# A third early pair of output tiles, another turn of the operand pools, and an earlier row-factor chain in a two-layer diffusion backbone

## The chip, the core and the metric

One core of one Trainium2 chip runs the whole kernel. The metric is device time in microseconds (us), the median of several runs. TensorE is called PE in the rows, VectorE DVE, ScalarE ACT, GpSimd POOL, and SyncE, which issues most transfers, SP.

## The reference

512 latent tokens and 256 context tokens of width 1024 pass through two layers. Layer 0 mixes tokens by windowed attention, layer 1 by a bidirectional gated linear recurrence over 8 heads of width 128. Each layer ends in a gated channel mixer of width 2816 (FFN0, FFN1). Everything is float32. After the recurrence, which is what the change touches, it computes, shortened:

```python
o = rms_norm(ox_f + flip(ox_b), o_gain) * silu(gate)      # per head of 128
x = x + g1 * (o.reshape(512, 1024) @ w_out)
h = rms_norm(x, norm2_g) * (1 + sc2) + sh2
gate, val = split(h @ w_up)                               # 1024 -> 2 x 2816
x = x + g2 * ((silu(dwconv3(gate)) * val) @ w_down)
```

## The kernel before

Activations lie transposed, features on the 128 partitions and tokens along the free axis. Each float32 product is made of three matmuls, with operands split into a rounded high part and the rest: `wh`*high, `wh`*low, `wl`*high. `mm_steps` (line 170) issues these three for each of the 8 feature blocks `k`.

**Weights.** `load_w` brings raw weights into one of two raw tiles of 1 MB (`wr`, transfers on SP's queue, line 95). Blocks of 512 columns are then converted, the high part by ScalarE (line 117), the rest by VectorE (line 118), into a pair of operand tiles (`wh`, `wl`). The pair comes from a list of pools, `self.wsp`, which is used in turn: `operand` takes the first pool and moves it to the end. `ws0` has 4 slots, `wsC`, `wsD` and `wsE` have 2 each. Conversions are issued with a higher priority than the program's order gives them.

**Recurrence.** For head `h`, `front` makes forget gates and queries, `back` values and gate, `scan` the recurrence. `scan` is a generator; between its steps the matmul steps of `back(h)` and `front(h+1)` are taken as filling. Behind head 7 the filling is `begin_out`: the output projection `ho` for tile pairs (0, 4) and (1, 5), each over heads 0 to 6 only, since head 7 isn't ready. A pair takes one of two double-bank tiles of pool `pj`. The scan's own banks are pool `sc` (`at`, `po`, `oss`, `oR`) and pool `lv` (`lv`, the fifth blocks of `kT` and `U`), two each. The end of a head is a chain: transposes `kT`, products `U`, states `S` on VectorE, outputs `po`, squares `osq` on ScalarE, sums `oss`, `rv` on VectorE, a power on POOL, `dg`, the broadcast `oR`, the product `oT`, and the split into `oh` by ScalarE and VectorE.

**Output projection and FFN1.** `hgrn_out` adds head 7 to the first two pairs and makes pairs (2, 6) and (3, 7) whole. Each tile is added to the stream by VectorE (`add_gated`, line 895), then scaled into `hn` (lines 362 and 363), squared (line 513) and added up in `acc` on POOL (line 515). FFN1 begins with `gate_plain` for its first block of 128 columns: 48 matmuls `pd` for the gate, 48 for the value, both without the row factor 1/rms. The generator `row_factor` makes that factor: first `nss` (sums over partitions of `acc`), `rv` and POOL's power, then `dg`, the broadcast `nR` and the copy into `R`. VectorE multiplies with `R` when it reads the products.

**Order.** The program gives each instruction a priority by its place. The builder's planner makes one fixed queue for each engine from that, before the run: an instruction that is ready by the planner's own time may pass one that isn't.

Of the kernel before, what the change touches and what calls it, by code (L numbers as in the profile page):

```python
# [8 lines left out]
F32 = mybir.dt.float32  # L9
# [7 lines left out]
P = 128  # L17
D = 1024
KT = D // P
# [53 lines left out]
class Kernel:  # L73
# [824 lines left out]
    def gate_plain(self, ft, ops, hn, G, gg, R, rows, half, tmp, bank):  # L898


        nc = self.nc
        act = lambda k: (hn[:, 0, k], hn[:, 1, k])
        cols = ((0, 256), (256, C0))
        for j, dst in enumerate((G[:, 1:1 + C0], gg)):
            ps = [bank("pd")[:, 0:hi - lo] for lo, hi in cols]
            for _ in self.mm_steps(ops[j], range(KT), act, [(o, lo) for o, (lo, _) in zip(ps, cols)]):
                pass
            for _ in rows:
                pass

            for o, (lo, hi) in zip(ps, cols):
                nc.vector.tensor_tensor(dst[:, lo:hi], o, R[:, lo:hi], op=ALU.mult)
# [119 lines left out]
    def hgrn(self, hn, R, acc, hb, pj, lv, sc):  # L1032
        nc, a = self.nc, self.a
        win = a["hgrn_w_in"][0]
        act = lambda k: (hn[:, 0, k], hn[:, 1, k])
        es = ExitStack()
# [7 lines left out]
        rows = self.row_factor(acc, False, h1, sc, "sc", 512, R, 1.0, (h1, "dg"))  # L1044
# [188 lines left out]
        wout = a["hgrn_w_out"][0]  # L1233
        part = [None, [], []]

        def split_o(h):
            oh = part[0]
            nc.scalar.activation(oh[:, 0, h], oT[:, h], AF.Copy)
            nc.vector.tensor_tensor(oh[:, 1, h], oT[:, h], f(oh[:, 0, h]), op=ALU.subtract)

        def begin_out():

            part[0] = oh = hb.tile([P, 2, KT, LAT], F32R, tag="hn", name="oh1")
            for dp in range(2):
                w = self.load_w([self.wcols(wout, d * P, P) for d in (dp, dp + 4)])
                ps = pj.tile([P, 1024], F32, tag="pj", name="ho")
                part[1].append(w)
                part[2].append(ps)
                for j in range(2):
                    out = [(ps[:, 512 * j:512 * j + 512], 0)]  # L1250
                    for k in range(KT - 1):
                        if dp == 0 and j == 0:
                            split_o(k)
                        yield from self.mm_steps(w[j], (k,), lambda k: (oh[:, 0, k], oh[:, 1, k]), out, k == 0, False)
# [4 lines left out]
        for h in range(KT):  # L1259
            def fill(h=h):  # L1260
                yield from back(h, ss[h])
                yield from (front(h + 1, ss[h + 1]) if h + 1 < KT else begin_out())

            rest = fill()
            for n in scan(h, ss[h]):
                for _ in range(n):
                    next(rest, None)
            for _ in rest:
                pass
# [4 lines left out]
    def hgrn_out(self, part, hn, acc, tmp, pj):  # L1274
        nc = self.nc
        self.shifts(1, 1, hn)
        wout = self.a["hgrn_w_out"][0]
        oh = part[0]
        act = lambda k: (oh[:, 0, k], oh[:, 1, k])
        for dp in range(KT // 2):  # L1280
            if dp < 2:
                w, ps, ks = part[1][dp], part[2][dp], (KT - 1,)
            else:
                w = self.load_w([self.wcols(wout, d * P, P) for d in (dp, dp + 4)])
                ps = pj.tile([P, 1024], F32, tag="pj", name="ho")
                ks = range(KT)
            for j in range(2):
                d = dp + 4 * j
                pd = ps[:, 512 * j:512 * j + 512]
                for _ in self.mm_steps(w[j], ks, act, [(pd, 0)], first=dp >= 2):  # L1290
                    pass
                self.add_gated(1, 2, d, pd, True)
            for d in (dp, dp + 4):
                self.scaled(1, 1, d, hn, True)
                self.square_acc(d, acc, True, tmp, "sg", first=(d == 0), eng=nc.gpsimd)
# [6 lines left out]
    def run(self, stop=99):  # L1302
        nc, a = self.nc, self.a
        top = ExitStack()
# [11 lines left out]

        xp = self.pool(top, "xp")
        self.xl = xp.tile([P, KT, LAT], F32, tag="xl", name="xl")
        self.wsp.append(self.pool(top, "wsC", 2))
        Rp = self.pool(top, "Rp", 1)  # L1320
        pjs = ExitStack()
        pj = self.pool(pjs, "pj", 2, PSUM)
# [6 lines left out]
        es = ExitStack()  # L1329
# [17 lines left out]
        rows = self.row_factor(acc, False, tmp, bk, "ps", 512, R, -1.0, (gp, "g"))  # L1347
# [23 lines left out]
        pjs.close()  # L1371
        pj = self.pool(pjs, "pj", 2, PSUM)
        es = ExitStack()
        self.wsp.append(self.pool(top, "wsD", 2, right=True))
        e2 = ExitStack()
        sc = self.pool(e2, "sc", 2, PSUM)
        lv = self.pool(e2, "lv", 2, PSUM)
        part = self.hgrn(hn2[0], R, accs[0], hb, pj, lv, sc)
# [13 lines left out]
        es = ExitStack()  # L1392
        tmp = self.pool(es, "tmpB", 2)
        acp = self.pool(es, "accB", 1)
        gp = self.pool(es, "gpB", 9)
        self.wsp.append(self.pool(es, "wsE", 2))
        bk = self.pool(es, "bkB", 8, PSUM)
        rows = self.row_factor(acc, True, tmp, bk, "ps", 512, R, -1.0, (gp, "g"))
        ost = {}
# [53 lines left out]
```

## Time and profile before

| | us |
|---|---|
| median of 3 runs | 1876.24 (1875.39 to 1877.27) |
| profiled execution | 1872.88 |
| its span, first to last instruction | 1871.1 |
| mean granted TensorE clock | 0.988 |

The span is what the rows of the trace lie in; the profiled execution's time is the number to which a sum of rows belongs, and the median is what a changed kernel is compared with. Times in rows are us from the span's start.

### The profile page before, as it was taken

To read this page: it belongs to the slowest core of one execution; us is meant where nothing else is said; L and a number is where in the kernel's file an instruction comes from. 1 tells how busy PE (TensorE), PEld (TensorE's weight loads), DVE (VectorE), ACT (ScalarE), POOL (GpSimd) and SP (SyncE) were. 2 spreads that over 40 slices of the span, in tenths; PEclk is the share of its full clock that TensorE was granted. 3 is DMA by queue.
4 is the path that set the end of the run, shared out by engine and by line. 5 is a ranking of instruction groups with operands and counts; after the bars stand their busy time and mean duration, and the time that the engine had idled before them with its cause. 6 is when DMAs were issued, how large, how long until landed. Compare 5 with 4: busy or idle time off the path is not lost.

```text
span 1871.1 us, 32302 instructions
## 1 busy us (share of the span) xinstructions
PE 1801.3 (96%) x13326; PEld 1576.9 (84%) x13326; DVE 1214.1 (65%) x2243; ACT 754.7 (40%) x1478; POOL 247.4 (13%) x233
## 2 busy tenths in 40 slices
PE   6999999998999999999998999999998999999998
PEld 4976786787888888989887888988886799899997
DVE  5575667466867686766777676777676655455462
ACT  4354555465534252434354333333332443233332
POOL 1233333103201000101013101111110200000000
PEclk9999999998999999999998999999999999999999
DMA  9204104232333333233313212122220332333321
GB/s 309 66 23 158 47 24 169 68 102 68 124 113 102 113 124 113 91 113 124 113 61 90 58 35 58 35 57 58 57 69 24 90 91 91 90 96 96 92 82 65
DMA packets 204416, 166.44 MB, mean 89 GB/s; under 512 B 5149, under 2 KB 198254, under 8 KB 199150
## 3 DMA queue, kind: packets, MB, share of 16 engines
q1 hardware_dynamic: 196608, 160.47, 27.8%
q10 hardware_dynamic: 7662, 3.92, 0.7%
q8 instruction: 105, 1.72, 0.4%
q14 instruction: 41, 0.34, 0.1%
HBM read 162.27 MB, written 2.10 MB: 88 GB/s over the span
## 4 chain that ended last, share of the span: by engine, by line
PE 87%; DVE 5%; DMA 4%; issue 2%; ACT 1%; POOL 1%; SPq 0%; ACTq 0%; POOLq 0%; DVEq 0%
PE dn L170 15%; PE pd L170 13%; PE pZ L188 8%; PE pf L170 8%; PE pV L188 4%; PE pjq L598 4%; PE pv L170 4%; PE ao L170 4%; PE ho L170 3%; PE pq L170 3%; PE pv L824 2%; PE pt L816 2%; PE ada L309 2%; PE pY L188 2%; PE pgate L170 2%; PE kv L598 2%
## 5 line engine op out<-in xcount | busy, mean ns | idle before, releaser
L117 ACT ACTIVATE wh<-wr 128x512 fp32r<-128x512 f32 (+1 forms) x320 | 193.0, 618 | 452.3 <-DMA wr<-in_ffn_w_up 74.8
L118 DVE TENSOR_TENSOR wl<-wr,wh 128x512 fp32r<-128x512 f32 (+1 forms) x320 | 223.6, 705 | 140.3 <-ACT wh L117 138.3
L170 PE MATMUL dn<-g,wh 128*128 128x512 f32 (+1 forms) x1056 | 263.3, 357 | 2.2 <-ACT g L995 2.2
L170 PE MATMUL pd<-hn,wh 128*128 128x256 f32 (+1 forms) x1408 | 227.3, 284 | 0.9 <-issue 0.9
L170 PEld LDWEIGHTS dn<-g,wh 128*128 128x128 f32 x1056 | 175.4, 189 | 32.7 <-ACT g L995 2.8
L170 PEld LDWEIGHTS pd<-hn,wh 128*128 128x128 f32 x1408 | 194.2, 190 | 2.5 <-issue 2.3
L188 PE MATMUL pZ<-hs,wh 128*128 128x386 f32 x704 | 185.2, 345 | 3.0 <-ACT wh L140 1.5
L170 PE MATMUL dn<-g,wl 128*128 128x512 f32 (+1 forms) x528 | 159.4, 356 | 0.0
L140 ACT ACTIVATE wh<-wr 128x512 fp32r<-128x512 f32 x132 | 81.6, 628 | 167.9 <-DMA wr<-in_ffn_w_up 47.4
L170 PE MATMUL pd<-hn,wl 128*128 128x256 f32 x704 | 141.8, 283 | 0.0
L188 PEld LDWEIGHTS pZ<-hs,wh 128*128 128x128 f32 x704 | 128.0, 190 | 15.7 <-ACT wh L140 4.4
L141 DVE TENSOR_TENSOR wl<-wr,wh 128x512 fp32r<-128x512 f32 x132 | 94.0, 717 | 53.6 <-ACT wh L140 53.5
L170 PE MATMUL pf<-hn,wh 128*128 128x512 f32 (+1 forms) x512 | 119.3, 349 | 9.7 <-DVE xc L1023 8.8
L188 PE MATMUL pZ<-hs,wl 128*128 128x386 f32 x352 | 119.4, 343 | 2.2 <-DVE wl L141 2.2
L926 POOL TENSOR_TENSOR gg<-gg,R 128x772 f32<-128x772 f32 x22 | 53.9, 2449 | 458.3 <-DVE gg L925 446.6
L170 PEld LDWEIGHTS pd<-hn,wl 128*128 128x128 f32 x704 | 109.0, 190 | 0.0
L1023 DVE SCALAR_TENSOR_TENSOR xl<-dn,mod,xl 128x512 f32<-128x512 f32 x72 | 53.9, 748 | 73.7 <-PE dn L170 73.6
L170 PEld LDWEIGHTS dn<-g,wl 128*128 128x128 f32 x528 | 87.4, 188 | 14.8
L170 PEld LDWEIGHTS pf<-hn,wh 128*128 128x128 f32 x512 | 80.9, 192 | 22.5 <-ACT wh L117 9.1
L188 PE MATMUL pV<-hs,wh 128*128 128x386 f32 x352 | 92.2, 341 | 5.0 <-ACT hs L392 5.0
L598 PE MATMUL pjq<-wh,hn 128*128 128x256 f32 x384 | 77.8, 291 | 0.0
L188 PEld LDWEIGHTS pZ<-hs,wl 128*128 128x128 f32 x352 | 66.7, 190 | 6.6 <-DVE gg L925 3.4
(299 smaller groups left out, 3807.1 us busy)
## 6 DMA issues: line engine op xcount, KB each, us to landing
wr<-in_ffn_w_up SPq DMA_DIRECT2D x88, 512.0 KB, 5.1
wada<-in_ada_w SPq DMA_DIRECT2D x40, 1024.0 KB, 4.8
wr<-in_hgrn_w_in SPq DMA_DIRECT2D x40, 512.0 KB, 4.2
ar<-in_ada_w SPq DMA_DIRECT2D x32, 256.0 KB, 7.1
wr<-in_ffn_w_down SPq DMA_DIRECT2D x16, 512.0 KB, 4.1
wr<-in_ffn_w_down SPq DMA_DIRECT2D x8, 896.0 KB, 4.7
wr<-in_attn_w_in SPq DMA_DIRECT2D x6, 1024.0 KB, 8.1
wr<-in_attn_w_out SPq DMA_DIRECT2D x8, 512.0 KB, 4.9
```

What stands on the lines that cost most here:

```text
L117: nc.scalar.activation(wh, src, AF.Copy)
L118: nc.vector.tensor_tensor(wl, src, f(wh), op=ALU.subtract)
L140: nc.scalar.activation(ops[i][0], src, AF.Copy)
L141: nc.vector.tensor_tensor(ops[i][1], src, f(ops[i][0]), op=ALU.subtract)
L170: nc.tensor.matmul(o, lhsT=wt, rhs=at[:, t0:t0 + o.shape[1]], start=(first and n == 0 and i == 0), stop=(last and n == len(ks) - 1 and i = ...
L188: self.nc.tensor.matmul(ps, lhsT=wt, rhs=at, start=(first and k == 0 and i == 0), stop=(k == nk - 1 and i == 2), skip_group_check=not first)
L309: nc.tensor.matmul(ps[32 * j:32 * j + 32, 0:512], lhsT=self.cs[:, k, :], rhs=raw[:, j * 512:(j + 1) * 512], start=(k == 0), stop=(k == KT ...
L598: nc.tensor.matmul(out, lhsT=x, rhs=y[:, wk], start=(start and k == 0 and j == 0), stop=(stop and k == KT - 1 and j == 2))
L816: nc.tensor.transpose(pt[:, j * P:(j + 1) * P], pr[j][:, b * P:(b + 1) * P], self.ident)
L824: nc.tensor.matmul(pv[a * HD:(a + 1) * HD, 0:256], lhsT=V[:, tl, g, :], rhs=pT[:, a * 256:(a + 1) * 256], start=(b == 0), stop=(b == len(t ...
L926: times = lambda eng, o, x, y: eng.tensor_tensor(o, x, y, op=ALU.mult)
L1023: nc.vector.scalar_tensor_tensor(x[:, d], o, self.modc(l, v, 5, d), x[:, d], op0=ALU.mult, op1=ALU.add)
```

## The change

Three edits. First, `begin_out` offers a third pair of tiles, (2, 6), over heads 0 to 3 only. Its two tiles go to two tiles of pool `lv`, its weights of heads 0 to 3 are loaded by themselves, and their operands come from `ws0` alone. `hgrn_out` loads the weights of heads 4 to 7 and completes the pair in the same banks. Second, the turn of the operand pools is set anew: `[ws0, wsC, ws0, wsD]` for the recurrence instead of `ws0, wsC, wsD`, and `wsE` behind these for FFN1. Third, `gate_plain` takes the first step of `row_factor` before its matmuls instead of behind the gate's.

```diff
@@ gate_plain
             ps = [bank("pd")[:, 0:hi - lo] for lo, hi in cols]
+            next(rows, None)
             for _ in self.mm_steps(ops[j], range(KT), act, [(o, lo) for o, (lo, _) in zip(ps, cols)]):
@@ begin_out
-            for dp in range(2):
-                w = self.load_w([self.wcols(wout, d * P, P) for d in (dp, dp + 4)])
-                ps = pj.tile([P, 1024], F32, tag="pj", name="ho")
+            for dp in range(3):
+                cols = [self.wcols(wout, d * P, P) for d in (dp, dp + 4)]
+                if dp < 2:
+                    w = self.load_w(cols)
+                    ps = pj.tile([P, 1024], F32, tag="pj", name="ho")
+                    ps = [ps[:, 0:512], ps[:, 512:1024]]
+                else:
+                    every, self.wsp = self.wsp, [self.ws0]
+                    w = [[op] for op in self.load_w([c[:, 0:4] for c in cols])[0]]
+                    self.wsp = every
+                    ps = [lv.tile([P, 512], F32, tag="lv", name="hol") for _ in range(2)]
...
-                    for k in range(KT - 1):
+                    for k in range(KT - 1 if dp < 2 else 4):
@@ hgrn_out
+            cols = [self.wcols(wout, d * P, P) for d in (dp, dp + 4)]
             if dp < 2:
                 w, ps, ks = part[1][dp], part[2][dp], (KT - 1,)
+            elif dp == 2:
+                w = [first + [op] for first, op in zip(part[1][dp], self.load_w([c[:, 4:8] for c in cols])[0])]
+                ps, ks = part[2][dp], range(4, KT)
             else:
...
-                for _ in self.mm_steps(w[j], ks, act, [(pd, 0)], first=dp >= 2):
+                for _ in self.mm_steps(w[j], ks, act, [(ps[j], 0)], first=dp >= 3):
@@ run
-        self.wsp.append(self.pool(top, "wsC", 2))
+        wsC = self.pool(top, "wsC", 2)
+        self.wsp.append(wsC)
...
-        self.wsp.append(self.pool(top, "wsD", 2, right=True))
+        wsD = self.pool(top, "wsD", 2, right=True)
+        self.wsp = [self.ws0, wsC, self.ws0, wsD]
...
-        self.wsp.append(self.pool(es, "wsE", 2))
+        self.wsp = [self.ws0, wsC, self.ws0, wsD, self.pool(es, "wsE", 2)]
```

## Rows read from the trace of the kernel before

**Rows 1.** The page, busy time in us, share of the span and instructions.

```profile
PE 1801.3 (96%) x13326; PEld 1576.9 (84%) x13326; DVE 1214.1 (65%) x2243; ACT 754.7 (40%) x1478; POOL 247.4 (13%) x233
```

**Rows 2.** Windows by stage: length, busy us of each engine, granted clock, DMA share.

```profile
1355.00:1406.00 51.00, 51.00 (x527) 45.67 (x526) 34.89 (x62) 17.26 (x36) 5.78 (x5) 1.00 0.22 63
...
1434.00:1450.00 16.00, 10.33 (x66) 7.66 (x64) 7.26 (x20) 2.65 (x6) 1.01 (x1) 0.86 0.00 1
1450.00:1480.00 30.00, 28.60 (x108) 21.54 (x108) 23.17 (x29) 15.89 (x29) 9.10 (x6) 0.90 0.38 105
1480.00:1500.00 20.00, 16.70 (x121) 15.57 (x121) 9.27 (x20) 7.61 (x11) 2.30 (x2) 0.91 0.19 54
1500.00:1600.00 100.00, 100.00 (x798) 98.21 (x798) 59.84 (x118) 38.56 (x60) 0.00 (x0) 1.00 0.32 96
...
1800.00:1871.00 71.00, 65.63 (x391) 57.32 (x390) 25.88 (x48) 18.13 (x31) 0.00 (x0) 0.99 0.21 69
```

**Rows 3.** Windows, the two seams cut finer, columns as in rows 2.

```profile
1434.00:1438.20 4.20, 4.02 (x32) 3.36 (x30) 3.23 (x11) 1.42 (x4) 0.00 (x0) 1.00 0.00 0
1438.20:1442.60 4.40, 3.21 (x24) 2.83 (x24) 1.74 (x6) 0.00 (x0) 0.00 (x0) 1.00 0.02 4
1442.60:1444.40 1.80, 1.05 (x8) 0.97 (x8) 0.78 (x2) 0.60 (x1) 0.00 (x0) 1.00 0.00 0
1444.40:1446.50 2.10, 0.00 (x0) 0.00 (x0) 0.83 (x2) 0.00 (x0) 1.01 (x1) 0.80 0.00 0
1446.50:1448.60 2.10, 2.04 (x2) 0.50 (x2) 0.00 (x0) 0.00 (x0) 0.00 (x0) 0.50 0.00 0
1448.60:1450.00 1.40, 0.00 (x0) 0.00 (x0) 0.69 (x1) 0.63 (x1) 0.00 (x0) 0.50 0.00 0
1450.00:1455.70 5.70, 5.66 (x12) 3.60 (x12) 4.42 (x9) 3.22 (x7) 0.00 (x0) 0.50 0.02 6
1455.70:1472.90 17.20, 17.17 (x73) 13.51 (x72) 12.90 (x15) 8.73 (x15) 5.82 (x4) 0.99 0.43 120
1472.90:1480.10 7.20, 5.84 (x24) 4.43 (x24) 5.85 (x7) 4.04 (x8) 3.27 (x2) 1.00 0.53 146
...
1487.80:1490.10 2.30, 0.00 (x0) 0.01 (x1) 1.04 (x3) 0.00 (x0) 1.02 (x1) 0.98 0.00 0
1490.10:1493.30 3.20, 3.18 (x9) 2.17 (x10) 0.47 (x2) 0.60 (x1) 0.00 (x0) 0.50 0.00 0
```

**Rows 4.** Windows, the instructions of tile ho alone.

```profile
1400.00:1434.00 34.00, 20.27 (x84) 15.47 (x84) 0.00 (x0) 1.00 0.18 51
```

**Rows 5.** Timeline of PE: start, us, line, operation, count, idle before.

```profile
1396.68 0.28 PE L1132 MATMUL lv<-Q,Y 128*32 128x32 f32 x6
...
1407.73 1.10 PE L546 MATMUL oR<-dg,cst 128*128 128x512 f32 x2 [0.42 <-DVE dg L543]
1408.67 1.05 PE L1113 MATMUL at<-q,KK 128*128 128x128 f32 x8
...
1446.55 2.04 PE L546 MATMUL oR<-dg,cst 128*128 128x512 f32 x2 [2.22 <-DVE dg L543]
...
1480.96 0.72 PE L170 MATMUL pd<-hn,wh 128*128 128x256 f32 x4 [0.89 <-issue]
```

**Rows 6.** Groups of VectorE by line, 1450 to 1482.5: busy us, mean ns, idle before.

```profile
L118 DVE TENSOR_TENSOR wl<-wr,wh 128x512 fp32r<-128x512 f32 x13 | 10.9, 847 | 4.4 <-ACT wh L117 4.4
L363 DVE SCALAR_TENSOR_TENSOR hn<-xl,gs,hn 128x512 fp32r<-128x512 f32 x8 | 8.6, 1079 | 0.2 <-ACT hn L362 0.2
L895 DVE SCALAR_TENSOR_TENSOR xl<-ho,mod,xl 128x512 f32<-128x512 f32 x8 | 5.9, 747 | 2.0 <-PE ho L170 1.8
```

**Rows 7.** Timelines of VectorE and of POOL, columns as in rows 5.

```profile
1455.59 0.74 DVE L363 SCALAR_TENSOR_TENSOR hn<-xl,gs,hn 128x512 fp32r<-128x512 f32 x1
...
1482.29 1.29 POOL L515 TENSOR_TENSOR acc<-acc,sq 128x512 f32<-128x512 f32 x1 [4.09 <-ACT sq L513]
```

**Rows 8.** Waits, 1098 to 1400: us in total, times, longest.

```profile
ACT wh L117 <- DMA wr<-in_hgrn_w_in: 42.7, 15, 5.7
```

More of the change, by code (lines that the diff above doesn't have):

```diff
@@ L1249, in begin_out @@
                 for j in range(2):
-                    out = [(ps[:, 512 * j:512 * j + 512], 0)]
-                    for k in range(KT - 1):
+                    out = [(ps[j], 0)]
+                    for k in range(KT - 1 if dp < 2 else 4):
                         if dp == 0 and j == 0:
@@ L1280, in hgrn_out @@
         for dp in range(KT // 2):
+            cols = [self.wcols(wout, d * P, P) for d in (dp, dp + 4)]
             if dp < 2:
                 w, ps, ks = part[1][dp], part[2][dp], (KT - 1,)
+            elif dp == 2:
+                w = [first + [op] for first, op in zip(part[1][dp], self.load_w([c[:, 4:8] for c in cols])[0])]
+                ps, ks = part[2][dp], range(4, KT)
             else:
-                w = self.load_w([self.wcols(wout, d * P, P) for d in (dp, dp + 4)])
+                w = self.load_w(cols)
                 ps = pj.tile([P, 1024], F32, tag="pj", name="ho")
+                ps = [ps[:, 0:512], ps[:, 512:1024]]
                 ks = range(KT)
@@ L1288, in hgrn_out @@
                 d = dp + 4 * j
-                pd = ps[:, 512 * j:512 * j + 512]
-                for _ in self.mm_steps(w[j], ks, act, [(pd, 0)], first=dp >= 2):
+                for _ in self.mm_steps(w[j], ks, act, [(ps[j], 0)], first=dp >= 3):
                     pass
-                self.add_gated(1, 2, d, pd, True)
+                self.add_gated(1, 2, d, ps[j], True)
             for d in (dp, dp + 4):
```

## The prediction

> **What bounds the kernel now.** The page comes first: TensorE is busy 96% of the span [rows 1]. A share that high is an average, so the stages come next. In the middle of the recurrence and in FFN1's body TensorE has no idle time at all: 51.00 of 51 us in a head, 100.00 of 100 us in FFN1 [rows 2]. Nothing that only starts operands earlier can gain there. Two seams are left: from 1434 to 1480 us, the end of the recurrence and its output projection, and from 1480 to 1493 us, the start of FFN1. FFN1's end (65.63 of 71 us busy) is not touched.
>
> The windows cut finer show what the two seams lose [rows 3]. Window less busy time is TensorE's idle time: 0.18 + 1.19 + 0.75 + 2.10 + 0.06 + 1.40 = 5.68 us from 1434 to 1450. That is head 7's last chain: states, `po`, square, row sums, POOL's power, `dg`, the broadcast `oR`, `oT`, the split into `oh`. Each link waits for the one before, and TensorE has nothing else left, because the 84 matmuls that `begin_out` offers (2 pairs x 2 tiles x 7 heads x 3) all ran before 1434 [rows 4]. The granted clock then falls: 0.80, then 0.50 from 1446.5 to 1455.7, the lower of its two levels, 1.2 GHz. So `oR` takes 2.04 us where head 6's took 1.10 [rows 5], 0.94 more, and 12 `ho` matmuls take 5.70 us. At the higher clock 73 of them take 17.20 us, 0.236 each [rows 3], so these 12 lose 5.70 - 2.83 = 2.87. The last 24 take 7.20 where 5.65 would do: 1.55 more, with a wait in front of them. The whole seam loses 5.68 + 0.94 + 2.87 + 1.55 = 11.0 us.
>
> The second seam: after the first 48 `pd` and the row sums `nss`, TensorE idles 2.30 us until `dg` is made, and the next 3.20 us run at 0.50 [rows 3], half of it lost: 1.6. Together 3.9 us.
>
> **The change, part by part.** *Third pair.* The work of `ho` does not change: 24 of its matmuls (2 tiles x 4 heads x 3), 24 x 0.236 = 5.65 us, may now run before head 7 is done. Two banks of `lv` receive them. These come free only after head 7's `U` tiles are read, if tiles of one tag are handed out in program order. The rows say so: `at` of head 7, ahead of its `lv` products in the program, ran at 1408.67, behind head 6's `oR`, while those products ran from 1396.68 on [rows 5]. Tag `sc` was the difference: `oR` stood first in its queue. So the third pair can't take a bank from the scan; it can start near 1438 us and finds 5.50 us of idle time in the five windows from 1438.2 to 1450.
>
> How much of 5.65 is hidden? At the most all; at the least 1.19, the gap in the state chain, if everything is put in it and the 4.46 left over pushes the chain back. The order of TensorE's queue is fixed beforehand, and the 84 matmuls were put as early as possible: they end at 1434 with 0.18 us idle behind them. I therefore let the first bank's 12 (2.83 us) go into the 1.19 us gap, 1.64 too much, and add 0.4 for the next gap of 0.75: the chain is late by 2.0, and 5.65 - 2.0 = 3.6 is hidden. Late behind it are `oss`, POOL's power, `dg` and `oR`, in that order, and then the last head's split.
>
> Busy gaps keep the clock up, which returns up to 0.94 at `oR` (taken) and up to 2.87 at the 12 matmuls (half taken, 1.4: 2 to 4 us of idle time may remain in front of them). Of the 1.55 I take half, 0.8: one wait for an eviction goes with the third pair's bank, one may stay. Sum of this part: 3.6 + 0.9 + 1.4 + 0.8 = 6.7 us; ends 1.2 (only the state gap is filled) and 11.0.
>
> Its loads: the pair's 1 MB is now two raw tiles of 0.5 MB each, so one more turn in a ring of two, with the same bytes; two transfers of 512 KB become four of 256 KB on SP's queue. FFN1's first raw tile then waits behind the second half, as it waited behind the whole. From 1455.7 to 1472.9 the DMA engines are 0.43 busy [rows 3]: I cost this at nothing; without that cover it is some us late, for operands that `pd` needs only behind the 84 `ho` that are left (84 x 0.236 = 19.8 us).
>
> *Operand pools in another turn.* Three pools with 4 + 2 + 2 slots in plain turn give a depth of 6 (the 2-slot pools come round every third operand); `ws0` taken twice gives 8, and 10 instead of 8 in FFN1. No matmul, conversion or byte is added. Cost and gain zero in the heads and FFN1's body, where TensorE has no idle time to give; the cover is TensorE's own backlog. The same turn leaves `ws0` free of the eight held operands' last halves, so the third pair's conversions need not wait.
>
> *1/rms chain sooner.* `nss`, `rv`, POOL's power now precede the gate's 48 `pd` in the program. At best the 3.9 us vanish: the chain runs under `pd`'s 5.7 us. At worst `nss` stands first in TensorE's queue and waits for POOL's last `acc`, 1482.29 + 1.29 = 1483.58 [rows 7], while `pd` could start at 1480.96 [rows 5]: 2.6 us lost with 48 `pd` queued behind it, 1.3 left. The lower end is not excluded, as a planned time may be early; `ho` passing unready work speaks for the upper. I take the middle, 2.6.
>
> Sum: 6.7 + 0 + 2.6 = 9.3 us. The profiled execution took 1872.88 us, 1.78 around its span of 1871.1, so it would take 1863.6. The median of the runs lies 3.36 above the profiled one: 1876.24 - 9.3 = **1866.9 us**.
>
> **The rivals.** *VectorE becomes the bound of the projection.* From 1450 to 1482.5 its three main groups take 10.9 + 8.6 + 5.9 = 25.4 us [rows 6]. Three conversions move ahead of 1450 (3 x 0.85): 22.9 remain. From the first eviction, 1452.4 as reckoned, with the 2.0 us it waits for TensorE, that is 1477.3 against 1482.5: 5.2 instead of 6.7, and 1876.24 - 5.2 - 2.6 = 1868.4. For it: L363 takes 1.08 us in the mean but 0.74 where POOL is idle [rows 6, 7], and POOL's adds crowd into a shorter stage. Against it: FFN1's conversions can slip.
> The Trainium skill (SBUF — State Buffer, Who interferes with whom) says that a VectorE instruction with two SBUF inputs contends with a GpSimd one that reads SBUF, and the loser fully blocks; L363 and POOL's add are such, and the trace agrees with its 1.08 against 0.74 us. By that rule the time would be this rival's 1868.4 rather than 1866.9.
>
> *The change doesn't do what it says*: the 24 matmuls stay behind the chain, or push it back by their own length. Then the first part is worth 1.2 to 1.5 and the sum 2.8 to 4.1: 1872.1 to 1873.4. For it: the planned gaps need not be the chip's. Against it: 84 such matmuls did move.
>
> *Slower*: deeper operands put ScalarE's conversions ahead of their data. From 1098 to 1400 us ScalarE already stood 42.7 us in 15 waits, the longest 5.7, for the recurrence's weights [rows 8]; the scan's `Y` and `kbt` queue behind such a wait, then TensorE. It is hidden today. It decides once a head costs (9.3 + 3.75) / 8 = 1.6 us of TensorE time; at 1.7 in each of 8 heads: 1866.9 + 13.6 = 1880.5. Against it: a raw tile freed sooner is also loaded sooner.
>
> **How the numbers follow.** A run of this kernel can tell about 0.2%, 3.75 us, from no change. Forecast 0.54, VectorE 0.14, no real fill 0.20, slower 0.08, smaller losses that cancel 0.04. Of the third case 0.08 still lies below 1872.5. So faster 0.54 + 0.14 + 0.08 = 0.76, same 0.12 + 0.04 = 0.16, slower 0.08. Low end: both parts at their best, 11.0 + 3.9 = 14.9, so 1861.5. High end: the third case's far end, 1873.5. Outside lie the slower case and the rarest mixes.
>
> **What would show it.** Right: `ho` matmuls between `U` and `oR`; `oR` near 1.1 us; the clock above 0.5 through the first `ho` of the last head; fewer than 90 `ho` after it; `nss` inside the first 48 `pd` and `nR` close behind them at full clock. Wrong: `po` or `oss` starting over 3 us later after `U` than now (overfilled); TensorE idle with VectorE full in the projection; `nss` ahead of `pd` behind a wait; idle TensorE inside a head.

## The result, and the profile after

The changed kernel took 1883.67 us (median of 8 runs, 1880.59 to 1887.68) against 1876.74 for the kernel before (8 runs, 1874.97 to 1879.46): a ratio of 1.0037, 95% interval 1.0028 to 1.0046. It is slower by 7 us; forecast were 9.3 us less, so the sign was wrong. Its profiled execution took 1880.59 us with a span of 1878.6.

TensorE does the same work in the same busy time. The page, as in [rows 1]:

```profile
PE 1802.4 (96%) x13326; PEld 1578.5 (84%) x13326; DVE 1217.7 (65%) x2243; ACT 756.9 (40%) x1478; POOL 251.1 (13%) x233
```

Windows over the two seams and FFN1's body, columns as in [rows 2]:

```profile
1434.00:1455.50 21.50, 16.85 (x113) 13.86 (x110) 9.20 (x22) 2.65 (x6) 1.01 (x1) 1.00 0.00 1
...
1456.40:1470.10 13.70, 13.66 (x51) 10.37 (x51) 12.11 (x19) 10.35 (x20) 3.35 (x2) 0.90 0.55 153
1470.10:1477.70 7.60, 0.00 (x0) 0.00 (x0) 7.60 (x8) 3.27 (x6) 4.53 (x4) 0.68 0.50 139
1477.70:1486.00 8.30, 8.25 (x24) 6.23 (x24) 2.56 (x4) 2.04 (x4) 1.58 (x1) 0.67 0.00 0
1486.00:1491.00 5.00, 1.48 (x10) 1.45 (x9) 2.29 (x5) 1.71 (x3) 1.26 (x1) 0.89 0.44 129
1491.00:1496.20 5.20, 5.20 (x25) 5.20 (x26) 0.85 (x2) 0.13 (x1) 1.02 (x1) 0.50 0.32 81
...
1510.00:1600.00 90.00, 90.00 (x746) 89.60 (x745) 56.36 (x111) 34.82 (x55) 0.00 (x0) 1.00 0.31 94
```

The chain of head 7 now runs at the higher clock up to the end of `oR`, but in the middle of the projection TensorE does nothing for 7.60 us while VectorE is full (7.60 of 7.60), and FFN1's first products run at 0.50. Two of these stretches are in the waits of TensorE, 1395 to 1510 (us in total, times, longest):

```profile
PE ho L170 <- DVE xl L895: 7.7, 1, 7.7
PE nss L524 <- POOL acc L515: 3.5, 1, 3.5
PE oR L546 <- DVE dg L543: 2.2, 1, 2.2
PE kT L1183 <- DVE K L1158: 1.7, 1, 1.7
```

The timeline of TensorE, columns as in [rows 5]:

```profile
1440.66 0.72 PE L170 MATMUL hol<-oh,wh 128*128 128x512 f32 x2
...
1445.41 0.40 PE L170 MATMUL hol<-oh,wl 128*128 128x512 f32 x1
1445.65 0.38 PE L1215 MATMUL po<-Q,S 128*128 128x128 f32 x2
...
1447.80 0.72 PE L170 MATMUL hol<-oh,wh 128*128 128x512 f32 x2
...
1450.68 0.95 PE L1226 MATMUL oss<-cst,osq 128*128 128x2 f32 x8
1453.85 1.10 PE L546 MATMUL oR<-dg,cst 128*128 128x512 f32 x2 [2.22 <-DVE dg L543]
1456.39 1.22 PE L170 MATMUL ho<-oh,wh 128*128 128x512 f32 x2 [1.44 <-ACT oh L1239]
...
1477.75 1.22 PE L170 MATMUL ho<-oh,wh 128*128 128x512 f32 x2 [7.66 <-DVE xl L895]
...
1489.56 1.55 PE L524 MATMUL nss<-cst,acc 128*128 128x2 f32 x8 [3.52 <-POOL acc L515]
1490.97 1.21 PE L170 MATMUL pd<-hn,wh 128*128 128x256 f32 x4
```

Between the first `po` and the next stand 21 `hol` products (1440.66 to 1445.65), and 12 more between the last `po` and `oss`: 33, not 24: nine of the 18 products for heads 4 to 6 of the pair, which the program has behind the chain, came along. The planner must have taken them as ready; e6 below, where they stand later in the program, has 24. `oR` takes 1.10 us again instead of 2.04 [rows 5].

Where an instruction stands on the clock of the span differs between profiles even where kernels agree: `at` of head 7 lies anywhere from 1432.2 to 1441.6 us, also among kernels that equal the one before up to there. So stretches are measured from that `at` (the last one in the program). Its row and that of `oss` in the kernel before:

```profile
1432.31 0.22 PE L1147 MATMUL at<-Q,K 128*64 128x64 f32 x1
...
1443.28 1.05 PE L1225 MATMUL oss<-cst,osq 128*128 128x2 f32 x8 [0.69 <-ACT osq L1219]
```

and the same `at` in the changed kernel, whose `oss` is shown above:

```profile
1434.27 0.22 PE L1148 MATMUL at<-Q,K 128*64 128x64 f32 x1
```

In us, worked out from the timelines (e1 to e16 are the experiments below): the chain is from `at` to the end of `oT`; the projection from there to the end of the last product into an output tile; "products in the chain" and "left behind it" count products into output tiles (in the first, of the third pair alone); "hn" is the mean ns of L363, "conv" that of L118, in the projection and just behind it; "first to 96th `pd`" is from start to start.

| kernel | median | ratio (95%) | products in the chain | chain | left behind it | projection, TensorE idle in it | conv, hn | to first `pd` | first to 96th `pd` | `at` to end |
|---|---|---|---|---|---|---|---|---|---|---|
| before | 1876.74 | 1 | 0 | 17.0 | 108 | 30.7, 2.1 | 847, 1079 | 0.9 | 17.3 | 438.8 |
| after | 1883.67 | 1.0037 (1.0028–1.0046) | 33 | 21.4 | 75 | 30.4, 8.4 | 932, 923 | 4.9 | 14.9 | 444.4 |
| e1 | 1877.85 | 1.0002 (0.9993–1.0011) | 0 | 17.0 | 108 | 30.7, 2.2 | 841, 1081 | 5.3 | 14.1 | 439.9 |
| e2 | 1879.72 | 1.0013 (1.0005–1.0022) | 0 | 16.4 | 108 | 33.2, 3.3 | 789, 1261 | 1.0 | 17.2 | 440.7 |
| e3 | 1881.86 | 1.0023 (1.0012–1.0034) | 42 | 23.5 | 66 | 30.1, 7.6 | 878, 1133 | 0.9 | 17.3 | 445.2 |
| e4 | 1883.85 | 1.0034 (1.0021–1.0047) | 33 | 22.3 | 75 | 30.2, 7.3 | 932, 921 | 1.0 | 17.4 | 443.7 |
| e5 | 1882.21 | 1.0035 (1.0021–1.0048) | 33 | 22.3 | 75 | 18.5, 0 | 937, 946 | 16.1 | 15.0 | 444.7 |
| e6 | 1881.83 | 1.0031 (1.0014–1.0047) | 24 | 19.7 | 84 | 29.8, 6.4 | 848, 1002 | 5.3 | 14.2 | 441.7 |
| e7 | 1872.45 | 0.9982 (0.9973–0.9991) | 0 | 17.0 | 108 | 30.7, 2.1 | 838, 1081 | 1.2 | 13.2 | 434.9 |
| e9 | 1882.29 | 1.0033 (1.0020–1.0046) | 42 | 23.5 | 66 | 30.4, 8.6 | 878, 1130 | 0.9 | 17.3 | 445.4 |
| e10 | 1876.62 | 1.0000 (0.9989–1.0011) | 33 | 21.4 | 75 | 30.3, 8.4 | 930, 919 | 1.0 | 13.2 | 438.8 |
| e11 | 1875.75 | 1.0000 (0.9991–1.0009) | 33 | 21.4 | 75 | 23.3, 2.5 | 687, 748 | 4.7 | 13.6 | 435.4 |
| e12 | 1878.58 | 1.0016 (1.0006–1.0027) | 0 | 16.1 | 108 | 35.5, 1.7 | 687, 749 | 3.4 | 13.9 | 441.4 |
| e13 | 1875.82 | 1.0002 (0.9993–1.0011) | 0 | 17.0 | 108 | 30.8, 2.1 | 688, 748 | 0.9 | 17.4 | 438.7 |
| e14 | 1873.64 | 0.9985 (0.9975–0.9994) | 12 | 17.1 | 96 | 31.8, 4.8 | 917, 922 | 0.9 | 13.2 | 435.9 |
| e15 | 1869.75 | 0.9976 (0.9966–0.9985) | 0 | 17.0 | 108 | 29.1, 0.9 | 687, 749 | 1.9 | 13.2 | 433.8 |
| e16 | 1867.75 | 0.9961 (0.9949–0.9973) | 12 | 16.5 | 96 | 26.9, 1.7 | 683, 744 | 0.9 | 13.2 | 430.0 |

After minus before, piece by piece: chain +4.4, projection -0.3, to the first `pd` +4.0, the first 96 `pd` -2.4, the rest -0.1, in all +5.6 of the 6.9 between the medians. One profile of a kernel may lie some us beside its median (3.9 below it in the kernel before, 6.6 above it in e13), so the last 1.3 us are not placed. Each experiment has its own runs of the kernel before beside it (medians 1876.15 to 1876.86), to which its ratio belongs.

### The profile page after: what moved, and what is told of

Its sections match the earlier page's. It is cut to its first block, busy times and chain, and to the rows that moved or that the text cites. A ratio compares the mean times of both kernels' runs of the same rounds, so it can differ in the third digit from the quotient of the medians.

```text
span 1878.6 us, 32348 instructions
## 1 busy us (share of the span) xinstructions
PE 1802.4 (96%) x13326; PEld 1578.5 (84%) x13326; DVE 1217.7 (65%) x2243; ACT 756.9 (40%) x1478; POOL 251.1 (13%) x233
## 4 chain that ended last, share of the span: by engine, by line
PE 87%; DVE 5%; DMA 4%; issue 2%; ACT 1%; POOL 0%; SPq 0%; ACTq 0%; DVEq 0%; POOLq 0%
PE dn L170 15%; PE pd L170 14%; PE pZ L188 8%; PE pf L170 8%; PE pV L188 4%; PE pjq L598 4%; PE pv L170 4%; PE ao L170 4%; PE pgate L170 3%; PE pq L170 3%; PE pv L824 2%; PE pt L816 2%; PE ada L309 2%; PE pY L188 2%; PE kv L598 2%; PE ho L170 2%
## 5 line engine op out<-in xcount | busy, mean ns | idle before, releaser
L118 DVE TENSOR_TENSOR wl<-wr,wh 128x512 fp32r<-128x512 f32 (+1 forms) x320 | 227.2, 715 | 133.5 <-ACT wh L117 120.7
```

What stands on the lines that cost most here:

```text
L118: nc.vector.tensor_tensor(wl, src, f(wh), op=ALU.subtract)
```

## The experiments

**The three edits alone, and two together.** e1_chain_only is the edit of `gate_plain` in the kernel before; e2_turn_only the three lines that set the turn of the pools; e3_pair_only the third pair with the old turn; e4_pair_and_turn the changed kernel without the edit of `gate_plain`.

> The kernel before with the earlier start of the 1/rms chain alone. Theory (the row sums stand first in TensorE's queue and hold the gate's 48 products back until GpSimd's last addition is done): the gate's products start some 3.7 us later than before, the idle time in front of the broadcast is gone, and the kernel is 0 to 2 us slower. Rival (the chain runs hidden under the products, as forecast): 2.6 to 3.9 us faster.

> The kernel before with the new turn of the operand pools alone. Theory (operands that are ready sooner let the planner put more projection products in front of the last head's upper levels, and the head's chain is pushed back): the heads 1 us faster in sum, the transposes of the last head 2 us later than before, the kernel 1 to 3 us slower. Rival (the turn costs and gives nothing): within 1 us of before.

> The kernel before with the third pair alone, in the old turn of the pools. Theory (the fill is put into the first two gaps of the chain, more than they hold, and afterwards the last pair's second tile waits for the eviction of its first, with nothing else left for TensorE): head 7's last products start 4 to 7 us later than before, one idle time of over 3 us stands in the middle of the last pair, and the kernel is 0 to 5 us slower. Rival (the third pair is a gain and another edit spoils it): 4 to 7 us faster.

> The changed kernel without the earlier start of the 1/rms chain. Theory (the chain's edit is worth only 1 to 2 us of the loss; most lies in the last head and in the wait of the last pair): 4 to 6 us slower than before. Rival (the row sums at the head of the queue are what costs): within 1 us of before.

No edit gains. 1.0002, 1.0013 and 1.0023 multiply to 1.0038, the changed kernel's 1.0037: within the intervals the loss is the sum of the edits, most of it the pair's. It doesn't follow that each does the same in company: the pair alone has 42 products in the chain, with the new turn 33. The pair's 5.0 us (1881.86 - 1876.86) lie at the end of the 0 to 5 expected, with one wait of 4.5 us for `xl`; e4 lost 7.0, more than the 4 to 6. In e2 the size came, but not at the place that its theory named: from `at` to `oss` there are 10.97 us as before, and the projection is 2.5 us longer. The eight `hn` take 1261 ns there instead of 1079, one more conversion stands in the stretch, and TensorE waits 2.6 us for `xl`; that these make all of the 2.5 isn't shown. In e1 `nss` stands first in TensorE's queue and `pd` waits behind it; waits of TensorE in e1:

```profile
PE nss L524 <- POOL acc L515: 3.5, 1, 3.5
```

**e5_last_pair_apart: the long wait taken away.** The 7.66 us end when `xl` has taken up a product: the last pair's two halves are one tile, and the second half's products wait until the first half has been read. In e5 they get two banks of the scan.

```diff
-                ps = pj.tile([P, 1024], F32, tag="pj", name="ho")
-                ps = [ps[:, 0:512], ps[:, 512:1024]]
+                ps = [sc.tile([P, 512], F32, tag="sc", name="hos") for _ in range(2)]
```

> The changed kernel, with the last pair's two output tiles in two banks of their own (the scan's sc banks) instead of the two halves of one tile. Theory (the second half's products wait for the eviction of the first half because both are one tile, and that eviction stands in VectorE's queue behind FFN1's conversions): the wait of 7.7 us in the middle of the last pair goes, and the low clock behind it; 4 to 8 us faster than the changed kernel, near the kernel before. Rival (VectorE alone sets the pace, and the products would only wait elsewhere): within 2 us of the changed kernel, with the idle time moved to the start of FFN1.

```profile
PE nss L524 <- POOL acc L515: 14.3, 1, 14.3
```

The rival held. The products end 12 us sooner (18.5 us without a gap), and the whole time stays within 2 us: TensorE waits 14.3 us at `nss` instead, because POOL's last addition ends 32.8 us behind `oT`, against 33.8 in the changed kernel. The long wait was where the delay showed, not its cause. e8_apart_only, the same edit in the kernel before, gave 1876.47 (1.0002, 0.9992 to 1.0012); there the wait of 1.4 us went, as its theory had it, another grew from 0.9 to 2.1, and the expected 1 to 2 us don't show in the medians.

> The kernel before with its last output pair in two banks of their own instead of the halves of one tile, nothing else. Theory (the wait of 1.4 us in front of the last tile is for the eviction of its other half): that wait is gone, 1 to 2 us faster. Rival (it waits for an operand's conversion): the wait stays, no change.

**e6_fill_capped and e9_half_pair: fewer products in the chain.** In e6 the pair's heads 4 to 6 come behind head 7's in the program, so that only the 24 are ready early. In e9 (the kernel before) only the first of the pair's tiles is offered early. The edit of e6:

```diff
-                ps, ks = part[2][dp], range(4, KT)
+                ps, ks = part[2][dp], (KT - 1, *range(4, KT - 1))
```

> The changed kernel, where the third pair's second part begins with head 7, so that only its 24 products of heads 0 to 3 can go into the last head's chain, not 33. Theory (every product beyond what a gap holds pushes the chain back by its own length, and pays for itself later): head 7's first output products start 2 us sooner than in the changed kernel; the total stays within 2 us of it, since the 9 products come back behind the chain. Rival (pushing the chain back is itself the loss): 2 us or more faster than the changed kernel.

> The kernel before with only the first of the third pair's two tiles offered early (12 products, heads 0 to 3) and the second made whole at the end; old turn of the pools, old place of the row factor. Theory (products put between the links of head 7's chain push it back, and each costs its place): the pair alone cost 5.1 us (1881.86 against 1876.8) with 42 of its products in the chain, so with some half of them about 2.5 us: 1879, and the first projection product of head 7 some 3 us later behind U than in the kernel before. Rival (the pair costs by its split operands or its late second part): as the whole pair, 1881.9, or, if only the second tile costs, no change.

e9 didn't change what it was meant to: its second tile, which no longer stood in the fill, was ready as well, and the planner put 42 products into the chain as in e3. It costs what e3 costs, so it tells nothing of half a pair. e6 does: `oss` stands 10.97 us behind `at` with none in the chain (before), 14.30 with 24, 16.41 with 33 (after), 18.51 with 42 (e3). From 24 on, nine more cost 2.1 us, 0.234 each: the full length of a product (0.236). The gaps swallowed 24 x 0.236 - 3.33 = 2.33 us, some ten products. e6's time, 1.8 us under the changed kernel's, lies too near the 2 us that were to part its theory from its rival, and the intervals overlap; the chain is 1.7 us shorter. The projection stays at some 30 us whether 108, 84, 75 or 66 products are left behind the chain.

**e7_sums_under_both and e10_sums_in_after: the second seam.** The first step of `row_factor` stands behind the second of eight blocks of the gate's products, and the rest, with the reads that need it, behind the value's. e7 is the kernel before with it, e10 the changed one (the edit shortened, arguments left out at `...`).

```diff
-            for _ in self.mm_steps(ops[j], range(KT), act, ...):
-                pass
+            for k, _ in enumerate(self.mm_steps(ops[j], range(KT), act, ...)):
+                if k == 1:
+                    next(rows, None)
+            done.append((dst, ps))
+            if ft == 0 and j == 0:
+                continue
             for _ in rows:
                 pass
-            for o, (lo, hi) in zip(ps, cols):
+            for dst, ps in done:
+                for o, (lo, hi) in zip(ps, cols):
```

> The kernel before, where the row sums follow the gate's second feature block in the program, and for the first block of FFN1 the rest of the 1/rms chain follows the value's products too, so that both halves' products can cover it. Theory (the chain's price at the start of FFN1 is the idle time in front of the broadcast and the low clock behind it; the edit failed because the row sums came first): the idle time of 2.4 us is gone, the clock stays at its higher level, 3 to 4 us faster than before. Rival (the products' banks or VectorE's reading of them take the time back): within 1 us.

> The changed kernel with the row factor's first step behind the second of the gate's eight blocks, and the rest of it behind the value's products. Theory (the seam at FFN1's start is a loss by itself, apart from the projection): 1883.7 - 4.4, what the same edit gave to the kernel before, = 1879.3, pd starting some 3 us sooner behind the projection and without the wait for POOL's sum. Rival (the projection's end, paced by VectorE, decides alone, since hn is late either way): 1883.7.

The time at FFN1's start was there to be had: 4.4 us in e7 (1876.83 - 1872.45), 7.0 in e10 against the changed kernel. `nss` stands behind some 40 `pd` in the queue, 96 `pd` take 13.2 us instead of 17.3 or 14.9, and the wait for POOL is gone. e10 gained more than the 4.4 expected: by the pieces 3.9 in front of the first `pd`, which the changed kernel had lost there, and 1.7 behind it, 5.6 of the 7.0.

**e11_no_pool_adds and e13_no_pool_adds_before: what paces the projection.** Six of POOL's seven additions are left out, so that 1/rms is not the right one; TensorE's work is the same.

```diff
-                self.square_acc(d, acc, True, tmp, "sg", first=(d == 0), eng=nc.gpsimd)
+                if d in (0, 7):
+                    self.square_acc(d, acc, True, tmp, "sg", first=(d == 0), eng=nc.gpsimd)
+                else:
+                    sq = tmp.tile([P, TOK], F32, tag="sg", name="sq", bufs=2)
+                    nc.scalar.activation(sq[:, 0:LAT], self.xl[:, d], AF.Square)
```

> The changed kernel with six of the seven sums of squares on POOL left out (the squares themselves are still made; so 1/rms is that of two tiles). Nothing of TensorE's work changes. Theory (VectorE paces the projection, and POOL's adds stretch its instructions): the eight hn fall from 0.92 to 0.74 us, the thirteen conversions from 0.93 to 0.80, together 3.1 us; from the end of oT to the last hn 29.5 instead of 32.7, and 1880.6 us in all. Rival (TensorE or the chain sets the stage): no change, 1883.7, VectorE merely idle longer.

> The kernel before with the same six of seven sums on POOL left out as in e11_no_pool_adds (1/rms is then that of two tiles). Theory (two limits in the projection: VectorE's, stretched by POOL's adds, and TensorE's own, which is 108 products x 0.236 = 25.5 us, some 3 us at the lower clock and 2.5 before the first): without the adds TensorE sets it, 2 us less: 1874.5; the third pair is then worth nothing even with VectorE free, since it pushes the chain back by as much as it takes off. Rival (POOL's adds cost the kernel before what they cost the changed one, 7.9 us): 1868.5, and the pair is a loss of some 7 us on any ground.

Groups of VectorE by line, as in [rows 6], in the changed kernel, 1456 to 1489:

```profile
L118 DVE TENSOR_TENSOR wl<-wr,wh 128x512 fp32r<-128x512 f32 x13 | 11.9, 932 | 4.0 <-ACT wh L117 4.0
L363 DVE SCALAR_TENSOR_TENSOR hn<-xl,gs,hn 128x512 fp32r<-128x512 f32 x8 | 7.3, 923 | 0.0
```

and in e11, 1453 to 1489:

```profile
L118 DVE TENSOR_TENSOR wl<-wr,wh 128x512 fp32r<-128x512 f32 x13 | 8.7, 687 | 1.8 <-ACT wh L117 1.8
L363 DVE SCALAR_TENSOR_TENSOR hn<-xl,gs,hn 128x512 fp32r<-128x512 f32 x8 | 5.9, 748 | 0.0
```

One line of the waits of TensorE in e11:

```profile
PE ho L170 <- DVE xl L895: 1.7, 1, 1.7
```

With POOL's adds gone the same instructions of VectorE take 14.6 instead of 19.2 us, the wait at the last pair falls from 7.7 to 1.7, and the projection from 30.4 to 23.3; the whole falls by 7.9 us, over twice the 3.1 expected. So VectorE, slowed by POOL, paced the changed kernel's projection. In the kernel before the same adds cost nothing: conversions and `hn` are just as short in e13, the projection is 30.8 long, and the 2 us that the theory expected from e13 didn't come. There TensorE sets it, with 108 products. The medians of e11 and e13 are the same, 1875.75 and 1875.82, each known to some 1.7 us. Their profiles, from `at`, put e11 3.3 us lower (435.4 against 438.7): 7.5 us come off the projection and 4.4 are given back in the chain. So with VectorE free the change gives back over half of what it takes off; whether it gives back all, as the theory had it, stays open.

**e12_sums_on_tensor: POOL's sums as products.** The kernel of e7, with the edit (shortened)

```diff
-                self.square_acc(d, acc, True, tmp, "sg", first=(d == 0), eng=nc.gpsimd)
+                nc.scalar.activation(sq, self.xl[:, d], AF.Square)
+                for i in range(NQ):
+                    nc.tensor.matmul(ss[:, 2 * i:2 * i + 2], lhsT=sq[:, i * P:(i + 1) * P], rhs=self.ones[:, 0:2],
+                                     start=(d == 0 and i == 0), stop=(d == KT - 1 and i == NQ - 1))
```

> The kernel of e7_sums_under_both with the squares summed by TensorE: four small products for each of the eight tiles, accumulated in a bank of the scan, in place of POOL's seven adds and the four products at the end; some 7 us more TensorE work inside the projection, POOL idle there. Theory (VectorE paces the projection): the eight hn fall from 1.08 to 0.74 us, 2.7 us, and the added products lie in TensorE's idle time: 1869.7. Rival (TensorE sets the stage): 1872.5 + 7 = 1879.5.

```profile
1461.10 2.73 PE L1307 MATMUL nss<-cst,sq 128*128 128x2 f32 x24
...
1486.79 1.05 PE L1307 MATMUL nss<-cst,sq 128*128 128x2 f32 x8 [1.33 <-ACT sq L1305]
```

The rival was right: VectorE's times fell as expected, but the projection grew from 30.7 to 35.5, since the added products take 4.4 us of TensorE there (not 7), and `nss`, with `pd` behind it, waits for the last squares. With 108 products left TensorE has no time to give, which e13 shows from the other side.

**e14_twelve_in_chain, e15_sums_on_vector, e16_twelve_and_vector: both limits moved.** e14 is e10 with 12 products in the chain; e15 is e7, and e16 is e14, with the sums on VectorE.

```diff
-                    for k in range(KT - 1 if dp < 2 else 4):
+                    for k in range(KT - 1 if dp < 2 else 2):
-                ps, ks = part[2][dp], range(4, KT)
+                ps, ks = part[2][dp], (KT - 1, *range(2, KT - 1))
@@ e15, e16
-                self.square_acc(d, acc, True, tmp, "sg", first=(d == 0), eng=nc.gpsimd)
+                self.square_acc(d, acc, True, tmp, "sg", first=(d == 0))
```

> The changed kernel with the third pair offered over heads 0 and 1 only (12 products), its other heads behind head 7's in the program, and the edit of e7_sums_under_both at FFN1's start. Theory (the chain's gaps hold 2.3 us, some ten products; VectorE paces the rest): oss is late by 0.5 instead of 5.4, the projection is not shorter, and the time is that of e7_sums_under_both, 1872.5, with 1 us either way. Rival (the pair pays once it isn't overfilled): 12 x 0.236 = 2.8 us less, 1869.7.

> The kernel of e7_sums_under_both with the seven sums of squares on VectorE instead of POOL. Theory (POOL's adds stretch the conversions by 0.12 and hn by 0.34 us each, 4.7 us in all; seven adds on VectorE cost 7 x 0.69 = 4.8): VectorE is as long busy as before, 1872.5; the eight hn fall to 0.75. Rival (what POOL's adds cost is more than that stretch, by its last add of 1.3 us and by waits behind blocked instructions): 1870 or less.

> The kernel of e14_twelve_in_chain with the seven sums of squares on VectorE. Theory: as e15_sums_on_vector, within 1 us of it, since the projection is VectorE's. Rival (with POOL idle TensorE's shorter backlog counts): 2 to 3 us less than e15_sums_on_vector.

In e14 the chain is 0.1 us longer than in the kernel before, and nothing is gained on e7 (1873.64 against 1872.45): TensorE waits 4.1 us for VectorE instead, as its theory had it. One line of the waits of TensorE in e14, and the same in e16:

```profile
PE ho L170 <- DVE xl L895: 4.1, 1, 4.1
```

```profile
PE ho L170 <- DVE xl L895: 1.0, 1, 1.0
```

Both medians of the kernels with the sums on VectorE are with their rivals: e15 is 2.7 us below e7, e16 2.0 below e15. But either time the intervals overlap, and from `at` the profiles of e7 and e15 differ by 1.1 only. Clear of noise is e16 against e14, which differ in the place of the sums alone: 5.9 us, with the intervals apart. Yet the seven adds cost VectorE 4.8 us, no less than the stretch by six of POOL's (19.2 - 14.6 = 4.6). Groups of VectorE in e16, 1453 to 1489:

```profile
L118 DVE TENSOR_TENSOR wl<-wr,wh 128x512 fp32r<-128x512 f32 x16 | 10.8, 684 | 2.7 <-ACT wh L117 2.6
L363 DVE SCALAR_TENSOR_TENSOR hn<-xl,gs,hn 128x512 fp32r<-128x512 f32 x8 | 5.9, 744 | 0.0
L515 DVE TENSOR_TENSOR acc<-acc,sq 128x512 f32<-128x512 f32 x7 | 4.8, 681 | 0.0
```

With POOL idle the shorter backlog counts (the wait for `xl` is 1.0 us, not e14's 4.1): e16's projection is 26.9 us against 29.1 in e15, and its 1867.75 beats both kernels, 8.6 us under the one before. What the third pair with the new turn is worth once it no longer overfills the chain and VectorE keeps up is 2.0 us by the medians (1869.75 - 1867.75; the two intervals overlap) and 3.8 by the profiles from `at`: a gain is likely, but not shown.

## Why the prediction was wrong

**What bounds the kernel.** TensorE's idle and slow time in the two seams, 11.0 and 3.9 us, was read rightly, and e7 got 4.4 out of the second. The mistake was to take the first seam's 11.0 as TensorE's to save. The projection had two limits of nearly one length, 30.7 by TensorE (e13: VectorE freed, 30.8) and 30.4 by VectorE beside POOL (the changed kernel: TensorE relieved, no shorter), and the page of before shows only the first. The 30.4 is no busy time: from the end of `oT` to the last `hn` VectorE is busy 24.6 of 32.7 us in the changed kernel. It counts where its queue is full, 7.60 of 7.60 us, while TensorE waits.

**The third pair** is the step that failed, in two of its terms. "The chain is late by 2.0, and 5.65 - 2.0 = 3.6 is hidden": `oss` came 5.44 us later and `oT` ended 4.4 later. I let only the first bank's 12 products be too many; 33 went in, and the gaps hold 2.33 us of them. The bound for this, 4.46 pushed back, was in the text, but there as what remains of a gain: it needed the projection to become shorter by all 24. It became shorter by 0.3. The 0.9 at `oR` did come (1.10 us) and lies in the 4.4. Of the terms for the clock behind it the 1.4 came at its place: the clock is at 0.50 for the first 2.81 us and 7 products, which lose some 1.2 us where 12 had lost 2.87. The 0.8 didn't: the last 24 products wait 7.66 us and then take 8.25 instead of 5.65. Neither made the projection shorter, since TensorE didn't set its length.

**The rival of VectorE** named the mechanism and sized it by its busy groups, 25.4 us less three conversions. The order of its queue counts too: it begins behind `oT`, 4.4 us later, and an eviction that TensorE waits for stands behind conversions and `hn` in order. The timeline of VectorE in the changed kernel, inside the 7.66 us:

```profile
1471.25 1.78 DVE L363 SCALAR_TENSOR_TENSOR hn<-xl,gs,hn 128x512 fp32r<-128x512 f32 x1
1472.95 3.42 DVE L118 TENSOR_TENSOR wl<-wr,wh 128x512 fp32r<-128x512 f32 x2
...
1476.96 0.74 DVE L895 SCALAR_TENSOR_TENSOR xl<-ho,mod,xl 128x512 f32<-128x512 f32 x1
```

The `hn` takes 1.78 us and the two conversions 3.42, where 0.75 and 1.4 are the measure in e11. The Trainium skill's rule (SBUF — State Buffer, Who interferes with whom), that a VectorE instruction with two SBUF inputs contends with a GpSimd one that reads SBUF, agrees with e11, 687 and 748 ns against 932 and 923. In the prediction that rule gave this rival's 1868.4; the mechanism came, the time didn't, since the chain's delay was not in it.

**The turn of the pools** was costed at nothing with TensorE's backlog as cover. That holds in the heads, where TensorE is busy 51.00 of 51 us as before; in the projection there is no such cover, and e2 lost 2.9 us (0.9 to 4.1 by its interval).

**The 1/rms chain.** The lower bound happened: `nss` stood first and waited 3.52 us. Its price was mis-sized: 1.3 us were to be left because the old idle time and low clock in front of and behind `nR` would go. They went (`nR` takes 1.02 us), but the same came at the head: behind the wait at `nss` the first 5.20 us of `pd` run at 0.50. In e1 nothing is left (+1.0 us, inside the interval around none).

**The other rivals.** "No real fill" had the chain pushed back by the pair's length, which is nearly what happened, but still credited 2.8 to 4.1 us from the clock and the second seam. Slower by late weights in the heads was not seen. Of the four signs that would show the forecast wrong, three came: `oss` late by over 3 us, TensorE idle with VectorE full, and `nss` ahead of `pd` behind a wait. But three signs for right came as well: products between `U` and `oR`, `oR` at 1.10 us, and 75 products left. They told that the edit does what it says, not that this gains time.

## What to carry to other kernels

Idle time on the engine that is busiest overall is a gain only if the stage's other engines would finish sooner as well: before costing a fill, work out each engine's own length of the stage, with the queue order and with its instructions at the durations they have beside their neighbours. Filling a chain of dependent steps is worth what its gaps hold, and every further instruction there costs its full length; in a queue planned beforehand, what else becomes ready with the fill goes in as well. Work that must wait for another engine belongs some instructions behind the start of the next stage, not at its head.

## What was not expected of the hardware

Beside seven adds of POOL, 1.3 to 1.8 us each, VectorE's conversions took 932 ns and its `hn` 923 in the mean; with six of the adds left out it was 687 and 748. The stretch isn't spread: in the changed kernel three of the thirteen conversions took 1.75 to 1.78 us and the other ten 0.68 to 0.69, and of the eight `hn` one took 1.78, one 1.14 and six 0.74 to 0.75. `xl` (L895), which reads one of its two inputs from a bank of products, was never stretched: one lay wholly beside an add and took 0.75 us. Taking six of the adds out shortened the changed kernel's projection by 7.1 us, more than the adds' share of VectorE's busy time (4.6 us) would say. The same seven adds on VectorE itself took 0.68 us each, and with 96 products left the whole was 5.9 us faster than with the adds on POOL, which had little else to do there (e16 against e14).
